# MLP layer two: the sixth block product of three chunks as seven small products for eight, and the second product by token tiles

## The chip, the cores and the metric

The kernel runs on one core of one Trainium2 chip. The metric is device time in microseconds (us) of that core; lower is better. The core has TensorE for matrix products (PE in the profile, PEld for its weight loads), VectorE (DVE), ScalarE (ACT), GpSimd (POOL) and SyncE (SP). DMAs are issued from the queues of SP, ACT and POOL. Each engine works through its own instructions in order; semaphores tie the engines to each other. PSUM has eight banks of 128 x 512 float32, into which TensorE writes.

## The reference, cut to what matters

The kernel computes one decoder layer for 512 tokens of width 2048. The change lies in the last part, a squared-ReLU MLP whose hidden width is 8192:

```
D_MODEL = 2048
SEQ = 512
D_FF = 4 * D_MODEL
...
        hn = rmsnorm(h, g_mlp[l])
        h = h + jnp.square(jax.nn.relu(hn @ w_ff1[l])) @ w_ff2[l]
    return rmsnorm(h, g_final)
```

"Layer two" below is the product with `w_ff2`: `u` (512 x 8192) times `w_ff2` (8192 x 2048), added to `h`.

## The kernel before, in words

**Precision.** Every float32 factor is split into a rounded part (`hi`, written by a ScalarE copy to the rounded type) and a remainder (`lo`, a VectorE subtraction). A product of two factors is three matmuls: hi by hi, hi by lo, lo by hi (`mm`, lines 1765 to 1767, each 128 x 128 by 128 x 512).

**Chunks and products.** Class `Mlp` does both layers. Layer two is cut into 8 chunks of 1024 hidden features. A chunk is a product of (512 tokens x 1024) by (1024 x 2048), done as a 2 x 2 x 2 block product with seven block products in place of eight (Winograd's form of Strassen's scheme). The products are numbered n = 0 to 6 in a chunk, and p counts them through both layers (`NP` = 56 in each). A block product is 256 tokens by 512 features by 1024 outputs: four weight tiles ("units", j = 0 to 3) of 128 x 1024, and for each of them two token tiles by two banks by three matmuls. So a unit is 12 matmuls, a product 48, a chunk 336.

**Where results go.** `USE` says for each n into which set of four PSUM banks it accumulates (X: four `mm` banks, for n = 0, 2, 4, 6; Y: three `st` banks and the `o` bank, for n = 1, 3 and, begun afresh, 5) and into which quarter of the output it is added after the product. A set is not cleared between its products: n = 2 goes on from n = 0, and so forth. `use2` (lines 1797 to 1804) adds the four banks to the residual rows in SBUF, four VectorE operations of 128 x 512, issued after the last unit of every product; the last of them waits for the last matmul.

**Weights.** `load` brings a unit from memory. For n = 0, 3 and 5 it is a plain load on SP's queue; for n = 1, 2, 4 and 6 it is a DMA on POOL's queue that adds the new block to a tile that is there already (the chain n = 0, 1, 2, 6 and the chain n = 3, 4), so such a DMA must wait until `low` has read the unit before it in its chain. `high` (line 1534) is the ScalarE cast of 128 x 1024, `low` (line 1539) the VectorE subtraction.

**Order of the work.** It is written out by hand in `run`. Before each unit i it calls `prep(i + FORE)` with `FORE` = 3, which puts into the queues: casts up to unit i + 4, remainders up to unit i + 3, loads up to unit i + 7. Then come, for the next product, the stationary factor (`stat` at j = 0: for n = 1 to 4 a VectorE sum of 128 x 1024, lines 1589 to 1595, and a ScalarE cast, line 1616; `stat_low` at j = 1: a VectorE subtraction, line 1621), the matmuls of the unit (`part`), and after j = 3 `use2`. On VectorE a product is thus: four remainders, for most n one sum, one `stat_low`, and four row additions, in that order, and nothing behind the row additions can start before the product's last matmul.

**Between the layers.** The results of layer one are transposed on TensorE into PSUM (`u_T`, line 1830), copied to one of four half tiles by ScalarE (`copies`, line 1839) and sent to memory by a DMA on ACT's queue (line 1840); layer two reads them back as its token factor. The last five of these copies fall into the first product of layer two and the start of its second. Its second product (p = `NP` + 1) begins a Y set whose fourth bank, `o`, was the last of the transposes' banks. `part` takes token tile 0 (banks 0 and 1) and then token tile 1 (banks 2 and 3) of each unit.

**Buffers.** Tiles of 128 x 1024 come from a list of 40 slots and 12 areas lent to it; `plain` takes the one that has been free for longer. A load waits until the slot's last reader is done.

Of the kernel before, what the change touches and what calls it, by code (L numbers as in the profile page):

```python
# [14 lines left out]
S, D, DFF, MEM = 512, 2048, 8192, 256  # L15
# [1443 lines left out]
class Mlp:  # L1459
# [14 lines left out]
    SIDE = ((0, 0), None, None, None, None, (0, 1), (1, 1))  # L1474
    CH = 8
    NP = 7 * CH
    TAG, TAG1 = "f2", "f1"
    FORE = 3
    ONE = False
    LAST = (5, 0, 1, 2, 3, 4, 6)  # L1480
    DONE = {0: (0, 0), 4: (1, 1)}

    def at(self, p):

        c, n = divmod(p - self.NP if p >= self.NP else p, 7)
        return c, self.LAST[n] if self.in_last(p) else n

    def in_last(self, p):
        return p >= 2 * self.NP - 7

    def begin(self, k):
        self.k, self.nc, self.W = k, k.nc, k.W
        self.raw, self.hl, self.chain, self.third = {}, {}, {}, {}
        self.S, self.sums, self.m = {}, {}, None
        self.nl = self.nh = self.no = 0
        self.units = 4 * (self.NP + 7 * self.CH)

    def __init__(self, k):
        self.begin(k)
# [11 lines left out]


    def load(self, i):
        p, j = divmod(i, 4)
        layer = p >= self.NP
        c, n = self.at(p)
        h, b = ((0, 0), (0, 1), (1, 1), (1, 1), (0, 1), (1, 0), (1, 0))[n]
        tag = (self.TAG, 8 * c + 4 * h + j, b) if layer else (self.TAG1, c, h, b, j)
        src = self.W.src(tag) if self.W.order is not None else None
        if n in (0, 3, 5):  # L1520
            t = self.k.slots.plain()
            (self.nc.gpsimd if self.ONE else self.nc.sync).dma_start(t, src)
            if n == 0:
                self.chain[j] = t
            elif n == 3:
                self.third[j] = t
        else:
            t = (self.third if n == 4 else self.chain)[j]
            self.nc.gpsimd.dma_start(t, src, accum_op=OP.add)  # L1529
        self.raw[i] = t  # L1530

    def high(self, i):
        t = HL(self.k.slots.get(), self.k.slots.get())
        self.nc.scalar.copy(t.hr, self.raw[i])  # L1534
        self.hl[i] = t

    def low(self, i):
        t, r = self.hl[i], self.raw.pop(i)
        self.nc.vector.tensor_sub(t.lr, r, t.hi)  # L1539
        if self.in_last(i // 4) and self.at(i // 4)[1] == 2:  # L1540
            self.load(i + 12)
        if self.at(i // 4)[1] >= 4:
            self.k.put(r)

    def loads(self, upto):
        while self.nl < upto:
            if not self.in_last(self.nl // 4) or self.at(self.nl // 4)[1] != 6:
                self.load(self.nl)
            self.nl += 1

    def prep(self, i):

        n = self.units
        self.loads(min(i + 2, n))
        while self.nh < min(i + 2, n):
            self.high(self.nh)
            self.nh += 1
        while self.no < min(i + 1, n):
            self.low(self.no)
            self.no += 1  # L1560
        self.loads(min(i + 2 + LOADS, n))


    def block(self, c, a):
        if c < self.CH:
            t = self.k.slots.plain()
            self.A[a] = [t]
            self.nc.sync.dma_start(t, self.k.d_u[c, a[1], a[0]].rearrange("p k n -> p (k n)"))

    def blocks(self, p):  # L1570

        if p < self.NP - 1:
            return
# [74 lines left out]
    def side(self, p, step):  # L1648

        if p > 7 * self.CH - 1:  # L1650
            return
# [25 lines left out]
    def run(self, out):  # L1677
        k = self.k
        if self.W.order is None:
            self.W.log += [("f1", c, h, b, i) for c in range(8) for h in range(2) for b in range(2) for i in range(4)]  # L1680
            self.W.log += [("f2", t, h) for t in range(DFF // 128) for h in range(2)]
            self.W.log += [(n, t, h) for n in ("wo", "w2") for t in range(KT) for h in range(2)]
            self.W.log += [("gs", c, h, b, i) for c in range(2) for h in range(2) for b in range(2) for i in range(4)]
        self.C, self.out = {}, out
        X = Y = None
        last = 2 * self.NP - 1
        for p in range(last):
            n, layer = self.at(p)[1], p // self.NP
# [5 lines left out]
            if n in (1, 5):  # L1694
                Y = [k.new_st() if p > 6 else k.new_mm() for _ in range(min(nb, 3))] + [k.new_o() for _ in range(nb - 3)]
            ps = (X, Y)[which]
            nh = 1 if p + 1 >= self.NP else 2
            for j in range(4):
                i = 4 * p + j
                self.copies()  # L1700
                self.prep(i + self.FORE)
                if j == 0:
                    self.blocks(p + 1)
                if j == 1 and p in (self.NP - 7, self.NP - 4, self.NP + 2, self.NP + 4):
                    self.res_in({-7: 0, -4: 1, 2: 2, 4: 3}[p - self.NP])
                if j % 2 == 0 and j // 2 < nh:
                    self.stat(p + 1, j // 2)
                if j % 2 and j // 2 < nh:
                    self.stat_low(p + 1, j // 2)
                while self.jobs and (self.jobs[0][0] <= i or i == 4 * self.NP + 3):  # L1710
                    self.jobs.popleft()[1]()
                if self.in_last(p):
                    if n in (1, 2) and j == 1:
                        self.gain(n - 1, 0)
                    if n == 4 and j in (1, 2):
                        for q in range(2):
                            self.square(j - 1, 2 + q)
                self.part(p, j, ps, range(2))
                if p == 0 and j < 2:
                    for d in (0, 1):  # L1720
                        self.x_in(12 + 2 * j + d, k.new_mm())
                if p == 0 and j == 3:
                    self.square(2, 2)
                    self.square(3, 2)
                if p == 1:
                    self.square(j, 3)
                if p == 2 and j == 2:
                    self.r = self.rstd(range(4), "rx3")
                if p == last - 14 and j == 0:
                    self.gain_rows()  # L1730
            if p == last - 1:
                self.prep(4 * last + 3)
# [8 lines left out]
        self.end(last, X, r)  # L1741

    def part(self, p, j, ps, ts):

        n = self.at(p)[1]
        B = self.hl[4 * p + j]
# [164 lines left out]

    def part3(self, p, j, i, ps):

        S, B, o = self.S[p, 0][0], self.hl[4 * p + j], 256 * j + 128
        self.mm(ps, S[:, o:o + 128], B[:, 512 * i:512 * i + 512], False, j == 3)

    def gain_rows(self):
# [36 lines left out]
class Gates(Mlp):  # L1954

    CH = 2
    ONE = True
    NP = 7 * CH
    TAG1 = "gs"
# [81 lines left out]
class Mixed(Mlp):  # L2041

    CH = 2
    NP = 0
    TAG = "wo"
    FORE = 4
    EARLY = 2
    ONE = True

# [119 lines left out]
class Out(Mlp):  # L2169

    CH = 2

    def in_last(self, p):
        return False
# [2 lines left out]
    HALF = 0.5  # L2177
    ONE = True
    TAG = "w2"
# [176 lines left out]
```

## Time and profile before

| | us |
|---|---|
| median of 3 runs | 2788.04 (2785.69 to 2788.9) |
| profiled execution, its own time | 2789.09 |
| its span, first to last instruction | 2787.3 |

| engine | busy us | share of the span | instructions |
|---|---|---|---|
| DVE | 2034.2 | 73% | 3217 |
| ACT | 1592.3 | 57% | 2670 |
| POOL | 530.9 | 19% | 796 |

The page of the profile gives busy time, the chain of work that ended last, and groups of instructions by line. Views of the trace used below are the waits (who waited for whom: total, times, longest), the timeline (start, duration, engine, line, operation, out<-in, count, and in brackets the idle time before it and who ended that), the windows (one line for a stretch: its length, then busy time and count of PE, PEld, DVE, ACT and POOL, the granted clock, the DMA share, GB/s) and the groups by shape. Tile names are the program's: `st`, `mm`, `o` are PSUM banks, `s`, `d` and `PP` are slots, `wts` is the weights in memory. In the timeline, a merged line (x4) shows the time from the first start to the last end.

### The profile page before, as it was taken

How to read it: one execution, taken by the hardware profiler on the slowest of the kernel's cores; microseconds unless marked ns; L12 is line 12 of the kernel's file. 1: busy time of each engine (PE TensorE's matmuls, PEld its weight loads, DVE VectorE, ACT ScalarE, POOL GpSimd, SP SyncE). 2: the span in 40 equal slices, each digit the busy share in tenths (PEclk: the TensorE clock that was granted, in tenths of full speed). 3: DMA queues.
4: the chain of work that ended last, by engine and by line, in shares of the span. 5: the costliest groups of instructions: out<-in, count | busy, mean ns of one | idle time of the engine just before them, and what ended most of it. 6: DMA issues, size and time to landing. Idle time of an engine off the chain costs nothing.

```text
span 2787.3 us, 37036 instructions
## 1 busy us (share of the span) xinstructions
PE 2765.3 (99%) x13428; PEld 2325.0 (83%) x13428; DVE 2034.2 (73%) x3217; ACT 1592.3 (57%) x2670; POOL 530.9 (19%) x796
## 2 busy tenths in 40 slices
PE   9999999999999999999999999999999999999998
PEld 8888889988888888888888888888888788888887
DVE  6347776766557886878866877777777788888888
ACT  5345556655557675556555766666666444444445
POOL 4021011011116232222200112111211121111111
PEclk9999999999999999999999999999999999999999
DMA  5331112222235798989814899888889998888986
GB/s 180 99 90 62 59 59 67 69 73 80 92 109 177 188 235 202 223 225 255 214 46 135 197 224 219 203 206 218 196 220 254 247 216 220 215 218 220 240 236 156
DMA packets 153383, 476.89 MB, mean 171 GB/s; under 512 B 15728, under 2 KB 40432, under 8 KB 153200
## 3 DMA queue, kind: packets, MB, share of 16 engines
q0 software_dynamic: 63616, 230.72, 39.8%
q1 hardware_dynamic: 71744, 226.25, 23.4%
q10 hardware_dynamic: 17840, 17.57, 1.9%
q8 instruction: 105, 1.72, 0.2%
q14 instruction: 78, 0.64, 0.1%
HBM read 443.01 MB, written 31.46 MB: 170 GB/s over the span
## 4 chain that ended last, share of the span: by engine, by line
PE 92%; DVE 3%; DMA 2%; ACT 2%; issue 1%; POOL 0%; DVEq 0%; ACTq 0%; POOLq 0%
PE mm L1767 10%; PE mm L1766 10%; PE mm L1765 10%; PE mm L437 9%; PE mm L439 8%; PE mm L438 8%; PE st L1767 7%; PE st L1765 7%; PE st L1766 7%; PE st L675 2%; PE o L1765 1%; PE o L1766 1%; PE o L1767 1%; PE st L438 1%; PE st L439 1%
## 5 line engine op out<-in xcount | busy, mean ns | idle before, releaser
L1765 PE MATMUL mm<-s,s 128*128 128x512 f32 x1392 | 545.4, 392 | 0.0
L1767 PE MATMUL mm<-s,s 128*128 128x512 f32 x1392 | 542.4, 390 | 1.1 <-DVE s L1621 1.0
L1766 PE MATMUL mm<-s,s 128*128 128x512 f32 x1392 | 541.8, 389 | 0.0
L1534 ACT CAST s<-d 128x1024 fp32r<-128x1024 f32 x272 | 282.3, 1050 | 245.7 <-DMA d<-wts 224.7
L437 PE MATMUL mm<-s,s 128*128 128x512 f32 (+5 forms) x1012 | 400.5, 396 | 0.0
L1539 DVE TENSOR_TENSOR s<-d,s 128x1024 fp32r<-128x1024 f32 x272 | 329.5, 1220 | 94.2 <-ACT s L1534 93.6
L1539 DVE TENSOR_TENSOR s<-s,s 128x1024 fp32r<-128x1024 f32 x252 | 304.9, 1221 | 105.4 <-ACT s L1534 103.3
L439 PE MATMUL mm<-s,s 128*128 128x512 f32 (+5 forms) x1012 | 381.6, 377 | 0.0
L438 PE MATMUL mm<-s,s 128*128 128x512 f32 (+5 forms) x1012 | 381.1, 377 | 0.0
L1534 ACT CAST s<-s 128x1024 fp32r<-128x1024 f32 x252 | 260.2, 1050 | 182.3 <-DMA s<-wts 161.5
L1765 PE MATMUL st<-s,s 128*128 128x512 f32 x920 | 360.6, 392 | 0.0
L1767 PE MATMUL st<-s,s 128*128 128x512 f32 x920 | 358.3, 389 | 0.0
L1766 PE MATMUL st<-s,s 128*128 128x512 f32 x920 | 358.1, 389 | 0.0
L1767 PEld LDWEIGHTS mm<-s,s 128*128 128x128 f32 x1392 | 261.3, 188 | 56.9 <-DVE s L1621 2.4
L1766 PEld LDWEIGHTS mm<-s,s 128*128 128x128 f32 x1392 | 261.4, 188 | 53.3
L1765 PEld LDWEIGHTS mm<-s,s 128*128 128x128 f32 x1392 | 261.4, 188 | 53.2 <-ACT s L1616 0.3
L1529 POOL DMA_DIRECT2D d<-wts x169 | 149.4, 885 | 813.1 <-DVE s L1539 662.3
L445 DVE TENSOR_TENSOR s<-s,s 128x512 fp32r<-128x512 f32 (+4 forms) x301 | 207.7, 700 | 94.9 <-ACT s L444 93.5
L444 ACT CAST s<-st 128x512 fp32r<-128x512 f32 (+4 forms) x249 | 112.3, 460 | 186.7 <-PE st L675 118.1
L439 PEld LDWEIGHTS mm<-s,s 128*128 128x128 f32 x1012 | 190.0, 188 | 32.6
L444 ACT CAST s<-s 128x512 fp32r<-128x512 f32 (+4 forms) x301 | 177.1, 603 | 59.6 <-PE mm L439 30.4
L437 PEld LDWEIGHTS mm<-s,s 128*128 128x128 f32 x1012 | 191.1, 189 | 20.9
(415 smaller groups left out, 4846.7 us busy)
## 6 DMA issues: line engine op xcount, KB each, us to landing
s<-wts SPq DMA_DIRECT2D x203, 512.0 KB, 3.7
d<-wts POOLq DMA_DIRECT2D x203, 512.0 KB, 8.2
s<-wts POOLq DMA_DIRECT2D x156, 512.0 KB, 8.2
d<-wts SPq DMA_DIRECT2D x69, 512.0 KB, 7.7
PP<-wts POOLq DMA_DIRECT2D x65, 512.0 KB, 8.5
d_u<-s ACTq DMA_DIRECT2D x64, 256.0 KB, 5.0
PP<-wts SPq DMA_DIRECT2D x27, 512.0 KB, 6.5
s<-d_u SPq DMA_DIRECT2D x16, 512.0 KB, 11.8
```

The costliest lines, as they stand in the source:

```text
L437: t.matmul(ps, a.hr, b.hr, start=first, stop=False)
L438: t.matmul(ps, a.hr, b.lr, start=False, stop=False)
L439: t.matmul(ps, a.lr, b.hr, start=False, stop=last)
L444: nc.scalar.copy(o.hr, src)
L445: nc.vector.tensor_sub(o.lr, src, o.hi)
L675: nc.tensor.transpose(ps[:rows, i * 128:i * 128 + 128], p, self.ident)
L1529: self.nc.gpsimd.dma_start(t, src, accum_op=OP.add)
L1534: self.nc.scalar.copy(t.hr, self.raw[i])
L1539: self.nc.vector.tensor_sub(t.lr, r, t.hi)
L1765: m(ps, a.hr, b.hr, start=first, stop=False, skip_group_check=True)
L1766: m(ps, a.hr, b.lr, start=False, stop=False, skip_group_check=True)
L1767: m(ps, a.lr, b.hr, start=False, stop=last, skip_group_check=True)
```

## The change

In chunks 0, 2 and 4 of layer two (`QUICK`) the sixth block product (n = 5) is itself done as a 2 x 2 x 2 block product of 128 tokens by 256 features by 512 outputs with seven sub-products. A sub-product is two weight half tiles by three matmuls, 6 matmuls; seven of them are 42.

- `sub_load` brings the four weight quarters in place of the four units, each as two DMAs of half a row, on SP's queue, nine units further ahead.
- `sum` puts four more VectorE operations of 128 x 1024 into the queue, the sums of quarters. Seven units, not four, then pass `high` and `low`. `prep`'s unit numbers run evenly over the chunk (`even`): 31 units in 55 steps of 6 matmuls.
- `stat_sums` makes four sums of 128 x 256 of the token factor on VectorE; `stat_hi2` casts them (ScalarE, 128 x 1024), `stat_lo2` is their remainder (VectorE, 128 x 1024).
- `swift` issues the sub-products: number 0 between units 2 and 3 of n = 4, numbers 1 to 5 in the place of n = 5, number 6 after the first unit of n = 6. Two results are carried on in PSUM: ScalarE copies bank a to b after sub-product 0 and b to f after sub-product 1, and later sub-products accumulate on the copies. Six row additions (`late2`), not four, are issued by `settled` a sub-product later.
- The second product of layer two (p = `NP` + 1) does token tile 0 of units 0, 1 and 2 before token tile 1 of unit 0.
- `Gates`, `Mixed` and `Out`, which inherit from `Mlp`, get `QUICK = ()` and keep their order.

```diff
+    QUICK = (0, 2, 4)
+    SUB = ((0, 0), (0, 1), (1, 1), (1, 0))
...
+    def even(self, p, j):
+
+        c = p - p % 7
+        if p < self.NP or not self.quick(c + 5):
+            return self.u0[p] + j
+        n = p % 7
+        t = 2 * (4 * n + j) if n < 5 else 40 + j if n == 5 else 47 + 2 * j
+        return self.u0[c] + 31 * t // 55
...
     def load(self, i):
-        p, j = divmod(i, 4)
+        p, j = self.U[i]
+        if i + 9 < len(self.U) and self.quick(self.U[i + 9][0]) and self.U[i + 9][1] < 4:
+            self.sub_load(*self.U[i + 9])
+        if self.quick(p):
+            return
...
+    def sum(self, i):
...
+        if j == 0:
+            B = [Q[p, i] for i in range(4)]
+            raw[u], raw[u + 3], raw[u + 5] = B[0], B[3], B[2]
+            raw[u + 2] = self.k.slots.plain()
+            v.tensor_sub(raw[u + 2], B[1], B[0])
+            raw[u + 4] = B[1]
+            v.tensor_sub(B[1], B[2], B[1])
+        elif j == 1:
+            raw[i] = self.k.slots.plain()
+            v.tensor_add(raw[i], Q[p, 1], Q[p, 0])
+            Q[p, 4] = raw[i]
+        elif j == 4:
+            raw[u + 6] = Q[p, 3]
+            self.turn4 = lambda: v.tensor_sub(Q[p, 3], Q[p, 3], Q[p, 4])
...
     def prep(self, i):
...
+        while self.nq < min(i + 4, n):
+            self.sum(self.nq)
+            self.nq += 1
...
-                self.prep(i + self.FORE)
+                self.prep(self.even(p, j) + self.FORE)
...
+                if j == 3 and p + 2 < last and self.quick(p + 2):
+                    self.stat_sums(p + 2)
+                if j > 1 and self.quick(p + 1):
+                    (self.stat_hi2 if j == 2 else self.stat_lo2)(p + 1)
+                self.settled()
...
-                self.part(p, j, ps, range(2))
+                if p == self.NP + 1:
+                    self.part(p, j, ps, [0])
+                    for i in (2, 3) if j == 3 else ():
+                        self.part(p, i - 1, ps, [1])
+                    if j > 1:
+                        self.part(p, j if j == 3 else 0, ps, [1])
+                else:
+                    self.part(p, j, ps, range(2))
+                if j == 2 and self.quick(p + 1):
+                    Y = [k.new_st() for _ in range(3)] + [k.new_o()]
+                    fast = self.swift(p + 1, Y)
+                    next(fast)
+                if p and j == 0 and self.quick(p - 1):
+                    next(fast, None)
...
+    def swift(self, p, ps):
...
+        plan = ((sub(0, 0), a, True, None, b), (com(1), b, False, (0, 1), f), (com(0), e, True, (1, 1), None),
+                (sub(0, 1), a, False, (0, 0), None), (com(2), f, False, (1, 1), None),
+                (com(3), e, False, (0, 1), None), (sub(1, 1), f, False, (1, 0), None))
+        for j, (l, o, start, at, to) in enumerate(plan):
+            self.prep(self.even(p, j) + self.FORE)
...
+            self.settled()
+            B = self.hl[self.u0[p] + j]
+            for q in range(2):
+                self.mm(o, l[q], B[:, 512 * q:512 * q + 512], start and q == 0, q == 1)
+            if to is not None:
+                nc.scalar.copy(to, o)
+            k.put(B.hi, B.lo)
+            if at:
+                r = self.row(*at)
+                self.late2.append(lambda o=o, r=r: v.tensor_add(r, o, r))
```

More of the change, by code (lines that the diff above doesn't have):

```diff
@@ L1494, in begin, with quick @@
         self.S, self.sums, self.m = {}, {}, None
-        self.nl = self.nh = self.no = 0
-        self.units = 4 * (self.NP + 7 * self.CH)
+        self.nl = self.nq = self.nh = self.no = 0
+        self.U, self.u0 = [], []
+        for p in range(self.NP + 7 * self.CH):
+            self.u0.append(len(self.U))
+            self.U += [(p, j) for j in range(7 if self.quick(p) else 4)]
+        self.units = len(self.U)
+        self.Q, self.late2 = {}, deque()
+    def quick(self, p):
+        return p >= self.NP and not self.in_last(p) and self.at(p)[1] == 5 and self.at(p)[0] in self.QUICK
+    def even(self, p, j):
[5 more added lines that the diff above has]
+        return self.u0[c] + 31 * t // 55
     def __init__(self, k):
@@ L1693, in run @@
                 X = [k.new_mm() if p else k.new_st() for _ in range(nb)]
-            if n in (1, 5):
+            if n == 1 or n == 5 and not self.quick(p):
                 Y = [k.new_st() if p > 6 else k.new_mm() for _ in range(min(nb, 3))] + [k.new_o() for _ in range(nb - 3)]
@@ L1697, in run @@
             nh = 1 if p + 1 >= self.NP else 2
+            if self.quick(p):
+                for _ in range(5):
+                    next(fast)
+                continue
             for j in range(4):
@@ L1731, in run @@
             if p == last - 1:
-                self.prep(4 * last + 3)
+                self.prep(self.units - 1)
                 r = self.rstd([0, 1], meanwhile=lambda: self.use2(p, ps))
@@ L1741, in run, with stat_sums @@
         self.end(last, X, r)
+    def stat_sums(self, p):
+        g = self.nc.vector
+        x = self.A[0, 1][0].rearrange("p (k n) -> p k n", k=4)
+        t = self.k.slots.plain()
+        s = [t[:, 256 * i:256 * i + 256].rearrange("p (k n) -> p k n", k=2) for i in range(4)]
+        a = {(h, kk): x[:, 2 * kk:2 * kk + 2, 128 * h:128 * h + 128] for h in range(2) for kk in range(2)}
+        g.tensor_add(s[0], a[1, 0], a[1, 1])
+        g.tensor_sub(s[1], s[0], a[0, 0])
+        g.tensor_sub(s[2], a[0, 0], a[1, 0])
+        g.tensor_sub(s[3], a[0, 1], s[1])
+        self.S[p, 1] = t
@@ new lines, in stat_hi2, with stat_lo2 @@
+    def stat_hi2(self, p):
+        t = self.S[p, 1]
+        x = HL(self.k.slots.get(), self.k.slots.get())
+        self.nc.scalar.copy(x.hr, t)
+        self.S[p, 1] = (x, t)
+    def stat_lo2(self, p):
+        x, t = self.S[p, 1]
+        self.nc.vector.tensor_sub(x.lr, t, x.hi)
+        self.k.put(t)
+    def swift(self, p, ps):
+        nc, k = self.nc, self.k
+        v = nc.vector
+        A, Z = self.S[p, 0][0], self.S[p, 1][0]
+        a, e, f, b = ps
+        sub = lambda t, kk: [A[:, 256 * (2 * kk + q) + 128 * t:256 * (2 * kk + q) + 128 * t + 128] for q in range(2)]
+        com = lambda i: [Z[:, 256 * i + 128 * q:256 * i + 128 * q + 128] for q in range(2)]
+        plan = ((sub(0, 0), a, True, None, b), (com(1), b, False, (0, 1), f), (com(0), e, True, (1, 1), None),
[3 more added lines that the diff above has]
+            self.prep(self.even(p, j) + self.FORE)
+            if j == 2:
+                self.blocks(p + 1)
+                self.stat(p + 1, 0)
+            if j == 4:
+                self.stat_low(p + 1, 0)
+            self.settled()
+            B = self.hl[self.u0[p] + j]
+            for q in range(2):
+                self.mm(o, l[q], B[:, 512 * q:512 * q + 512], start and q == 0, q == 1)
[5 more added lines that the diff above has]
+                self.late2.append(lambda o=o, r=r: v.tensor_add(r, o, r))
+            if j == 6:
+                k.put(A.hi, A.lo, Z.hi, Z.lo)
+            yield
@@ L1956 @@
     CH = 2
+    QUICK = ()
     ONE = True
@@ L2043 @@
     CH = 2
+    QUICK = ()
     NP = 0
@@ L2171 @@
     CH = 2
+    QUICK = ()
     def in_last(self, p):
```

37 lines of the change are left out of this document (32 added, 5 removed).

## The prediction

> **What bounds the kernel now.** I read the page first, then the waits of PE, then the windows of single chunks of layer two, then the timeline of VectorE and ScalarE inside them.
>
> ```profile
> span 2787.3 us, 37036 instructions
> PE 2765.3 (99%) x13428; PEld 2325.0 (83%) x13428; DVE 2034.2 (73%) x3217; ACT 1592.3 (57%) x2670; POOL 530.9 (19%) x796
> PE 92%; DVE 3%; DMA 2%; ACT 2%; issue 1%; POOL 0%; DVEq 0%; ACTq 0%; POOLq 0%
> ```
>
> TensorE is busy throughout and is the chain that ends last, so a matmul fewer, or a wait more, moves the end one for one. The next view is the window of chunk 2 of layer two, from its first matmul to that of chunk 3.
>
> ```profile
> 2320.75:2396.91 76.16, 76.16 (x337) 63.06 (x336) 63.67 (x68) 34.68 (x35) 14.08 (x16) 1.00 0.89 221
> ```
>
> PE has no gap in it: 336 matmuls of its own in 76.16 us are 0.2267 us each, a unit of 12 is 2.72, a product of 48 is 10.88. The clock is full. VectorE is busy for 63.67 us; it has 12.5 us to spare in a chunk, ScalarE 41.
>
> The one wait of PE that the change aims at is in the second product of layer two (waits of PE, then the timeline):
>
> ```profile
> PE o L1765 <- ACT s L1839: 2.2, 1, 2.2
> ```
> ```profile
> 2176.82 0.39 PE L1765 MATMUL st<-s,s 128*128 128x512 f32 x1
> 2180.58 0.58 ACT L1839 COPY s<-o 128x512 f32<-128x512 f32 x1 [5.83 <-DMA d_u<-s]
> 2181.22 0.50 PE L1765 MATMUL o<-s,s 128*128 128x512 f32 x1 [2.19 <-ACT s L1839]
> 2201.07 0.39 PE L1765 MATMUL st<-s,s 128*128 128x512 f32 x1
> ```
>
> The product starts at 2176.82, comes to the `o` bank after 9 matmuls, and waits 2.19 us for ScalarE's copy out of it, which itself waited for a DMA to free its half tile. The last row is the first matmul of n = 3 of chunk 0.
>
> **The change part by part.**
>
> *Matmuls.* Three products lose 6 matmuls each: 3 x 6 x 0.2267 = 4.08 us, 1.36 a chunk.
>
> *Second product.* Token tile 0 of three units (18 matmuls) and the first bank of tile 1 (3) now lie ahead of the `o` bank: 2176.82 + 21 x 0.2267 = 2181.58, and the copy ends at 2181.16. The wait of 2.19 goes, with 0.4 us to spare; bounds 0 to 2.19, should the DMA land later.
>
> So at best 6.27 us go. What is added is work for VectorE. Its prices, by groups of shape (the last two rows, of 128 x 256 and of ScalarE's copies, are of other stages):
>
> ```profile
> L1539 DVE TENSOR_TENSOR s<-d,s 128x1024 fp32r<-128x1024 f32 x106 | 127.7, 1219 | 21.3 <-ACT s L1534 21.1
> L1589 DVE TENSOR_TENSOR s<-s,s 128x1024 f32<-128x1024 f32 x5 | 6.1, 1219 | 0.0
> L1804 DVE TENSOR_TENSOR s<-s,mm 128x512 f32<-128x512 f32 x48 | 32.1, 686 | 10.7 <-PE mm L1767 10.7
> L1306 DVE TENSOR_TENSOR s<-mm,s 128x256 f32<-128x256 f32 x4 | 1.7, 418 | 0.9 <-PE mm L439 0.9
> L1839 ACT COPY s<-o 128x512 f32<-128x512 f32 x61 | 35.2, 577 | 5.8 <-DMA d_u<-s 5.8
> ```
>
> Back to back they cost less than they last, as the timeline of n = 3 and n = 4 of chunk 2 shows:
>
> ```profile
> 2349.12 1.22 DVE L1539 TENSOR_TENSOR s<-d,s 128x1024 fp32r<-128x1024 f32 x1
> 2351.55 2.73 DVE L1804 TENSOR_TENSOR s<-s,mm 128x512 f32<-128x512 f32 x4 [1.21 <-PE mm L1767]
> 2354.20 1.22 DVE L1539 TENSOR_TENSOR s<-s,s 128x1024 fp32r<-128x1024 f32 x1
> 2355.33 1.22 DVE L1595 TENSOR_TENSOR s<-d,s 128x1024 f32<-128x1024 f32 x1
> 2356.47 1.22 DVE L1539 TENSOR_TENSOR s<-d,s 128x1024 fp32r<-128x1024 f32 x1
> 2362.29 1.23 DVE L1539 TENSOR_TENSOR s<-d,s 128x1024 fp32r<-128x1024 f32 x1 [2.20 <-ACT s L1534]
> 2363.43 1.88 DVE L1802 TENSOR_TENSOR s<-st,s 128x512 f32<-128x512 f32 x3
> 2365.23 0.68 DVE L1802 TENSOR_TENSOR s<-o,s 128x512 f32<-128x512 f32 x1
> 2365.90 2.36 DVE L1539 TENSOR_TENSOR s<-s,s 128x1024 fp32r<-128x1024 f32 x2
> ```
> ```profile
> 2353.39 0.39 PE L1765 MATMUL st<-s,s 128*128 128x512 f32 x1
> ```
>
> Wide operations (128 x 1024) start 1.135 us apart (2354.20, 2355.33, 2356.47). Four row additions that need not wait take 2365.90 - 2363.43 = 2.47, 0.62 each. A small sum lies between 0.34 (its 0.42 less the overlap of 0.085) and 0.42; I take 0.34, as its operands are all in SBUF. VectorE cannot run ahead over a product's end: its row additions wait for the last matmul, and it is free 0.81 us after the next product's start (2353.39 to 2354.20).
>
> In one of the three chunks VectorE gets: three more remainders, one remainder of the token sums, four sums of quarters (8 x 1.135 = 9.1), four small sums (1.35), two more row additions (1.2): 11.65 us. 63.67 + 11.65 = 75.3, and PE would need only 74.80. Most of it falls into n = 3 and n = 4, where the 12.5 us to spare are not to be had.
>
> So I follow VectorE's queue from T, the start of n = 3, by the order in which `run` fills it (units counted in the chunk, `even` applied):
>
> - n = 3: remainder 16, sum for n = 4, two sums of quarters, remainder 17, `stat_low`, third sum, remainders 18 and 19, four small sums; four row additions of n = 3
> - n = 4: remainders 20, 21, 22, `stat_low`, remainder 23, fourth sum, remainders 24, 25, `stat_lo2`; four row additions of n = 4
> - n = 5: remainder 26, addition of sub-product 1, remainder 27, addition of sub-product 2, which frees bank e
>
> PE needs `stat_lo2` for the third matmul of sub-product 1: T + 10.88 + 8.16 (three units) + 1.36 (sub-product 0) + 2.72 (unit 3) + 0.45 = T + 23.57. VectorE has by then 18 wide operations, the small sums and four row additions to do: T + 0.81 + 20.4 + 1.35 + 2.5 = T + 25.1. PE waits 1.5 us. Sub-product 5 accumulates on bank e, so it must wait for the addition that reads it: without waits PE is there at T + 28.56. VectorE: 20 wide, 10 row additions, the small sums: T + 0.81 + 22.7 + 6.2 + 1.35 = T + 31.06. **All in all PE waits 2.5 us per chunk** (of which 1.5 are the first wait), against 1.36 saved: +1.14 in chunks 2 and 4. After that there is room: n = 6 has no sum, and the next chunk is an ordinary one.
>
> In chunk 0 PE is 2.19 us earlier, but VectorE is not, since remainder 11 of n = 2 is tied to a DMA:
>
> ```profile
> 2189.87 2.00 ACT L1534 CAST s<-d 128x1024 fp32r<-128x1024 f32 x2 [2.01 <-DMA d<-wts]
> 2191.43 1.22 DVE L1539 TENSOR_TENSOR s<-d,s 128x1024 fp32r<-128x1024 f32 x1
> ```
>
> Its cast starts at 2189.87 because the DMA lands then; the remainder can start at 2190.95; seven wide operations (remainders 11 to 15, sum and `stat_low`) and four row additions bring VectorE to 2201.37. T is 2201.07 - 2.19 = 2198.88, so VectorE is free at T + 2.49, not T + 0.81: 1.68 later. PE waits 4.18: -1.36 - 2.19 + 4.18 = +0.63. **Most of the second product's gain is given back in the same chunk.**
>
> Sum: 0.63 + 1.14 + 1.14 = +2.9 us.
>
> *What I cost at nothing.* ScalarE: four more casts and three copies a chunk, some 6 us of its 41. The copy a to b must end before T + 23.12; ahead of it in its queue lie nine casts after that of unit 19.
>
> ```profile
> 2364.82 2.00 ACT L1534 CAST s<-s 128x1024 fp32r<-128x1024 f32 x2 [2.56 <-DMA s<-wts]
> 2367.67 2.95 ACT L1534 CAST s<-s 128x1024 fp32r<-128x1024 f32 x3
> ```
>
> At 0.95 us apart they end at about 2365.8 + 9 x 0.95 = 2374.4, T + 21.0; with 0.58 (the copies' row above; between 0.3 and 1.05) T + 21.6, 1.5 us in time, and the copy b to f has two sub-products as cover. The half loads carry the same bytes and start nine units (24 us) earlier on SP's queue; the loads of n = 3 stand behind them there. If that cover fails, it shows as a late remainder (second rival).
>
> [...]
>
> **The rivals.**
>
> *One: it is hidden.* If VectorE gets through n = 3 and n = 4 without PE waiting, 4.08 + 2.19 = 6.3 us go: 2782.8 in the profiled execution. For it: VectorE idles 12.5 us a chunk. Against: that idle time lies ahead of n = 3, behind row additions that wait for PE. Half of it would be 2786.
>
> *Two, slower: the fourth DMA of n = 4.* In the new order remainder 19 stands ahead of n = 3's row additions and of everything that sub-product 0 needs, so each us by which its data come after VectorE is ready is a us of PE. VectorE is ready for it at T + 0.81 + 8 x 1.135 = T + 9.89. Before, it started at 2365.90 in chunk 2 (T + 9.89 = 2363.28) and, in chunks 0 and 4, here:
>
> ```profile
> 2215.52 1.23 DVE L1539 TENSOR_TENSOR s<-s,s 128x1024 fp32r<-128x1024 f32 x1 [0.17 <-ACT s L1534]
> 2517.59 2.35 DVE L1539 TENSOR_TENSOR s<-s,s 128x1024 fp32r<-128x1024 f32 x2
> 2505.71 0.39 PE L1765 MATMUL st<-s,s 128*128 128x512 f32 x1
> 2355.82 0.87 POOL L1529 DMA_DIRECT2D s<-wts  x1 [4.20 <-DVE s L1539]
> ```
>
> If the landings stay, 2.6 us are added in chunk 2, 2.0 in chunk 4 (T = 2505.71), 5.1 in chunk 0: +9.7, together +12.6 or 2801.7. It is slower by more than can be told from nothing once a third of this comes true. Against: the last row, where that DMA's issue in chunk 2 waits for remainder 15, which now stands ahead of n = 2's row additions, behind the remainder of 2349.12, and can start at 2350.3 and not 2354.20; and the loads of n = 5 have left that stretch.
>
> *Three: full durations.* At 1.22 and 0.69 instead of 1.135 and 0.62 the sum grows by 20 x 0.085 + 10 x 0.07 = 2.4 a chunk, and 0.9 more in chunk 0: +8.1, together +11, 2800.1.
>
> *Four: the change does not do what it says.* The `o` bank comes free later, as half loads share the DMA engines with the transposes' writes, and PE waits there as before. By the sum for chunk 0 this costs next to nothing more, as VectorE sets the time there: 2792.
>
> **How the numbers follow.** The profiled execution took 2789.09 (span 2787.3, 1.8 around it), 1.05 more than the median of the runs, 2788.04. The forecast is 2789.09 + 2.9 = 2792.0 in its terms, 2791.0 as a median; its own range, with small sums and overlaps at their bounds, 2788 to 2795. Chances: forecast 0.47, hidden 0.2, the DMA 0.23, full durations 0.05, no effect on the wait 0.05. Two in a thousand, 5.6 us, is about what a measurement can tell from no change here: faster means below 2782.5, which only the whole of the first rival reaches, 0.1; slower means above 2793.6, most of the second and third rivals, 0.28; between them 0.62. The range from 2783 to 2799 leaves out the whole of the first rival and the worst of the others.
>
> **What would show it.** In the changed profile: 18 matmuls fewer, no wait of 2.2 on the copy at `o`; new waits of PE on VectorE of about 1.5 us at sub-product 1 and 1 us at sub-product 5 in each of the three chunks, some 1.7 more in chunk 0; VectorE without idle time from the start of n = 3 until sub-product 5. If PE shows no such waits, my queue is wrong; if VectorE waits at remainder 19 for a cast that waits for a DMA, it is the second rival; if wide operations start 1.22 apart, the third.

## The result, and the profile after

The kernel after takes 2805.01 us (median of 6 runs, 2803.23 to 2806.87), the kernel before 2788.47 in the same series: a ratio of 1.0060, with a 95% interval from 1.0047 to 1.0073. It is 16.5 us slower, where 2.9 us were forecast, and it lies outside the range. The profiled execution of after took 2803.23 us, the fastest of its six; what the profile shows is that one execution.

The page of after, its span and busy time:

```profile
span 2801.5 us, 37069 instructions
PE 2768.3 (99%) x13410; PEld 2322.6 (83%) x13410; DVE 2064.4 (74%) x3259; ACT 1606.9 (57%) x2688; POOL 531.0 (19%) x796
```

The 18 matmuls are gone (13428 to 13410), and the span is 14.2 us longer. The windows of chunks 0, 2 and 4 of after, each from its first matmul to that of the next chunk, say where:

```profile
2164.18:2247.76 83.58, 79.64 (x349) 64.53 (x348) 72.65 (x80) 42.49 (x47) 13.22 (x15) 0.98 0.88 225
2323.92:2405.29 81.37, 77.70 (x331) 62.76 (x330) 72.97 (x81) 38.54 (x40) 13.21 (x15) 0.98 0.83 206
2481.45:2563.16 81.71, 77.65 (x331) 62.82 (x330) 72.81 (x81) 38.60 (x40) 13.21 (x15) 0.98 0.84 205
```

Before, these chunks took 80.58, 76.16 and 76.16. The differences, 3.00, 5.21 and 5.55, are 13.76 of the 14.2 us. The chunks between them still take 76.16. What PE waits for in after (its waits from 2100 us to the end):

```profile
PE st L1919 <- DVE s L1690: 8.7, 3, 2.9
PE st L1917 <- DVE d L1886: 1.8, 3, 0.6
PE o L1982 <- ACT s L1991: 0.8, 1, 0.8
PE mm L1919 <- DVE s L1690: 0.6, 2, 0.4
PE st L1918 <- DVE s L1594: 0.3, 2, 0.2
```

The wait of 2.2 at the `o` bank in the second product is gone (L1982 is the transposes of layer one's results). In its place PE waits 2.9 us in each of the three chunks for a `stat_low` (L1690), and 0.6 for the addition that frees bank e (L1886). Both are VectorE's. The next two fences show where VectorE lost its time in chunk 2: its timeline, and the matmul with which n = 3 starts, T.

```profile
2343.32 1.23 DVE L1594 TENSOR_TENSOR s<-PP,s 128x1024 fp32r<-128x1024 f32 x1 [1.27 <-ACT s L1589]
2347.08 1.22 DVE L1594 TENSOR_TENSOR s<-d,s 128x1024 fp32r<-128x1024 f32 x1 [2.53 <-ACT s L1589]
2348.22 1.88 DVE L1954 TENSOR_TENSOR s<-st,s 128x512 f32<-128x512 f32 x3
...
2358.63 2.47 DVE L1956 TENSOR_TENSOR s<-s,mm 128x512 f32<-128x512 f32 x4
2361.02 1.22 DVE L1594 TENSOR_TENSOR s<-s,s 128x1024 fp32r<-128x1024 f32 x1
```
```profile
2356.56 0.39 PE L1917 MATMUL st<-s,s 128*128 128x512 f32 x1
```

VectorE comes to n = 2's row additions at 2358.63, 1.9 us after their matmuls, and is free at 2361.02, T + 4.46; the forecast had T + 0.81. The idle time lies earlier, ahead of remainders whose casts are late. Summed over the products n = 0 to 2 of chunk 2 (waits of VectorE in before, then in after):

```profile
DVE s L1539 <- ACT s L1534: 1.1, 1, 1.1
```
```profile
DVE s L1594 <- ACT s L1589: 5.4, 4, 2.5
```

ScalarE, which makes the casts, in turn waits for add-on DMAs (its waits in the same two stretches, before, then after):

```profile
ACT s L1534 <- DMA d<-wts: 7.7, 4, 3.0
```
```profile
ACT s L1589 <- DMA d<-wts: 12.1, 4, 5.3
ACT s L1589 <- DMA PP<-wts: 1.6, 1, 1.6
```

The DMA view of 30 us from the same place of the chunk, before and then after, has busy tenths of the DMA engines in 40 slices, what they moved, and per kind of issue the median time to landing:

```profile
DMA  9979943799999999999999999950000966068679
DMA packets 1398, 5.10 MB, mean 170 GB/s; under 512 B 160, under 2 KB 160, under 8 KB 1395
d<-wts POOLq DMA_DIRECT2D x5, 512.0 KB, 6.9
```
```profile
DMA  9999999999999999999999999999999950000001
DMA packets 2097, 6.59 MB, mean 220 GB/s; under 512 B 240, under 2 KB 240, under 8 KB 2093
d<-wts POOLq DMA_DIRECT2D x4, 512.0 KB, 10.0
```

After has no gap for 24 us, then moves next to nothing for 5: half loads, the loads of n = 3 and the add-ons of n = 1 and n = 2 stand in one heap, and an add-on takes 10.0 us to land and not 6.9 (medians of the rows shown).

### The profile page after: what moved, and what is told of

Its sections match the earlier page's. It is cut to its first block, busy times and chain, and to the rows that moved or that the text cites. A ratio compares the mean times of both kernels' runs of the same rounds, so it can differ in the third digit from the quotient of the medians.

```text
span 2801.5 us, 37069 instructions
## 1 busy us (share of the span) xinstructions
PE 2768.3 (99%) x13410; PEld 2322.6 (83%) x13410; DVE 2064.4 (74%) x3259; ACT 1606.9 (57%) x2688; POOL 531.0 (19%) x796
## 5 line engine op out<-in xcount | busy, mean ns | idle before, releaser
L1589 ACT CAST s<-s 128x1024 fp32r<-128x1024 f32 x285 | 294.9, 1049 | 228.2 <-DMA s<-wts 193.8
L1594 DVE TENSOR_TENSOR s<-s,s 128x1024 fp32r<-128x1024 f32 x285 | 344.6, 1220 | 108.3 <-ACT s L1589 107.9
L1589 ACT CAST s<-d 128x1024 fp32r<-128x1024 f32 x247 | 257.0, 1050 | 213.4 <-DMA d<-wts 190.8
L1594 DVE TENSOR_TENSOR s<-d,s 128x1024 fp32r<-128x1024 f32 x247 | 299.6, 1219 | 96.9 <-ACT s L1589 96.0
L1919 PEld LDWEIGHTS mm<-s,s 128*128 128x128 f32 x1392 | 262.1, 188 | 58.5 <-DVE s L1690 3.7
L1918 PEld LDWEIGHTS mm<-s,s 128*128 128x128 f32 x1392 | 262.6, 189 | 53.8
L1917 PEld LDWEIGHTS mm<-s,s 128*128 128x128 f32 x1392 | 262.5, 189 | 53.4
L1552 POOL DMA_DIRECT2D d<-wts x153 | 135.3, 884 | 794.1 <-DVE s L1594 555.4
L439 PEld LDWEIGHTS mm<-s,s 128*128 128x128 f32 x1012 | 190.0, 188 | 34.2 <-DVE s L448 1.7
L1919 PEld LDWEIGHTS st<-s,s 128*128 128x128 f32 x920 | 172.9, 188 | 45.8 <-DVE s L1690 9.7
```

The lines of the kernel that those rows point to most:

```text
L439: t.matmul(ps, a.lr, b.hr, start=False, stop=last)
L1917: m(ps, a.hr, b.hr, start=first, stop=False, skip_group_check=True)
L1918: m(ps, a.hr, b.lr, start=False, stop=False, skip_group_check=True)
L1919: m(ps, a.lr, b.hr, start=False, stop=last, skip_group_check=True)
```

## The experiments

All chunk lengths are read from the trace as above. "Time" is the median where there were several runs, else the one run. Chunk 0 starts between 2162.5 and 2166.4 us in these profiles: what lies ahead of it differs by up to 4 us, so the chunks are the better measure.

| kernel | time | chunk 0 | chunk 2 | chunk 4 |
|---|---|---|---|---|
| before | 2788.47 | 80.58 | 76.16 | 76.16 |
| after | 2805.01 | 83.58 | 81.37 | 81.71 |
| tiles_only, tiles_again | 2786.69, 2787.86 | 78.36, 78.09 | 76.16 | 76.16 |
| no_sums | 2797.55 | 83.35 | 80.31 | 77.47 |
| loads13 | 2802.61 | 85.26 | 80.62 | 81.01 |
| lead_late | 2806.36 | 85.24 | 81.61 | 82.82 |
| loads4 | 2793.78 | 80.62 | 79.46 | 78.65 |
| low_first | 2806.12 | 86.12 | 81.75 | 80.87 |
| pool_sums | 2833.56 | 93.57 | 90.48 | 91.51 |
| combo | 2820.42 | 90.22 | 87.42 | 85.92 |
| loads4_no_sums | 2788.97 | 79.20 | 78.53 | 75.20 |
| early_token | 2791.93 | 78.96 | 77.71 | 76.67 |
| by_due | 2792.47 | 79.40 | 77.85 | 75.81 |

The letters of the theories hold within one expectation each.

**The second product alone** (tiles_only, and tiles_again in five rounds).

```diff
-    QUICK = (0, 2, 4)
+    QUICK = ()
```

> The second product by token tiles alone (QUICK is empty). Theory A, the wait at the o bank was all there was to it: chunk 0 of layer two takes 80.58 - 2.19 = 78.4 us from its first matmul to that of chunk 1, the other chunks 76.16, the kernel 2.2 us less than before. Theory B, the first weights of layer two, tied to DMAs, hold PE up later in the same chunk: chunk 0 stays above 79.5 and PE waits for VectorE there.

> The second product by token tiles alone (QUICK empty), once more, in five rounds. The run of three rounds gave 2786.69 and a ratio of 0.9993, its interval from 0.9983 to 1.0003. Theory: the wait of 2.19 us at the o bank is gone and nothing else moves, so 2.2 us less, a ratio of 0.9992; an interval of five rounds may or may not leave 1 out. If the 2.2 us came only by chance in that run, chunk 0 would take 80.5 us again.

Chunk 0 takes 78.36 and 78.09 in place of 80.58, 2.2 and 2.5 us less, and the other chunks stay at 76.16. The gain is there in the trace. In the times it cannot be told from nothing: ratios 0.9993 (0.9983 to 1.0003) and 0.9996 (0.9987 to 1.0005).

**The sums of quarters left out** (no_sums; quarters go in their place, all the rest of the change stays).

```diff
-            v.tensor_sub(raw[u + 2], B[1], B[0])
-            raw[u + 4] = B[1]
-            v.tensor_sub(B[1], B[2], B[1])
+            raw[u + 2] = raw[u + 4] = B[1]
```

> The changed kernel without its four sums of weight quarters (the quarters themselves go in their place; the result is another): 4.5 us of VectorE work fewer in each of the three chunks, same matmuls, same loads, same casts. Theory A, VectorE's queue sets the time from the start of n = 3 on: the three chunks lose some 2 us against their matmuls (6.6 in the changed kernel), chunk 2 takes 76.5 to 77.5 us, not 81.4. Theory B, PE waits for something that does not depend on the amount of VectorE work (the order of the token factor, bank copies, DMAs): chunk 2 stays at 80 us or more.

Chunk 4 comes down by 4.2 us, chunk 2 only by 1.1, chunk 0 by 0.2. That the 4.2 is near the 4 x 1.135 that the sums cost is in part luck. VectorE is free 0.9 us earlier there (T + 3.90 and not T + 4.81), though the sums lie behind that point. From there to the addition that frees bank e it takes 3.4 us less: the sums' 4.5 less 1.20 that it now idles ahead of remainder 19. In chunk 2 VectorE stands 3.01 us idle there, since the add-on DMA is late, and in chunk 0 a wait of 2.4 us at the second product's `o` bank is back:

```profile
PE o L1908 <- ACT s L1982: 2.4, 1, 2.4
```

So the sums are a part of the loss, and late DMAs another.

**Half loads thirteen units ahead** (loads13).

```diff
-        if i + 9 < len(self.U) and self.quick(self.U[i + 9][0]) and self.U[i + 9][1] < 4:
-            self.sub_load(*self.U[i + 9])
+        if i + 13 < len(self.U) and self.quick(self.U[i + 13][0]) and self.U[i + 13][1] < 4:
+            self.sub_load(*self.U[i + 13])
```

> The half loads start 13 units ahead, not 9, so that they land before the add-on DMAs of n = 1 and n = 2. Theory A, the half loads delay these add-ons, and through them remainders 10 and 11, so that VectorE comes late to n = 3: VectorE ends its row additions of n = 2 about 1 us after the start of n = 3 (4.5 in the changed kernel), chunk 2 takes 77 to 78.5 us, not 81.4. Theory B, VectorE is late for another reason: chunk 2 stays within 1 us of 81.4.

Within 0.8 us of after in chunks 2 and 4, and chunk 0 worse: by its numbers theory B. But loading the halves still earlier does not clear the stretch. All eight are now issued ahead of chunk 2, and the loads of n = 3 stand among the add-ons of n = 1 and n = 2 instead; VectorE is free at T + 3.71 in chunk 2 and T + 4.10 in chunk 4. The run does not tell the two theories apart.

**The queue's lead put off** (lead_late).

```diff
         n = p % 7
+        if n < 3:
+            return self.u0[p] + j
```

> The lead of `even` begins at n = 3, so remainders 10 and 11 stand behind the row additions of n = 1, as before the change. Theory A, the DMAs are late and VectorE waits for them in either order: VectorE is free 3 to 4 us after the start of n = 3, chunk 2 takes 80 to 81.5 us. Theory B, the order is at fault, a remainder that waits for a DMA ahead of row additions that need not: VectorE is free at most 1.5 us after that start, chunk 2 takes 77.5 to 78.5 us.

No gain. VectorE is free at T + 3.24 in chunk 2, inside theory A's 3 to 4 us, but one more wide operation now lies behind that point: from there to the addition that frees bank e it takes 31.76 us and not 30.48. That `prep` runs ahead of the ordinary order in the first three products is not what costs the time.

**Half loads four units ahead** (loads4).

```diff
-        if i + 9 < len(self.U) and self.quick(self.U[i + 9][0]) and self.U[i + 9][1] < 4:
-            self.sub_load(*self.U[i + 9])
+        if i + 4 < len(self.U) and self.quick(self.U[i + 4][0]) and self.U[i + 4][1] < 4:
+            self.sub_load(*self.U[i + 4])
```

> The half loads are issued four units ahead, not nine, so that they stand behind the loads of n = 3 on SP's queue and not between them. Theory A (VectorE comes to n = 3 late because the add-on DMAs of n = 1 and n = 2 share the DMA engines with half loads and loads of n = 3 issued at 2321 to 2335 us): the add-ons of n = 1 and n = 2 land as early as before, VectorE is free at about T + 0.8 in chunk 2 in place of T + 4.46, the first wait of PE falls from 2.9 to 0.5 at most, and chunks 2 and 4 take 77.3 to 78.5 us in place of 81.4 and 81.7: about 2797. Rival B (the order of the loads is not what makes the add-ons late; the faster running ahead of the queue is): VectorE still free at T + 4 or later, chunks 81 to 82, about 2804. If the halves land too late, VectorE idles ahead of the first quarter sum, and that shows there.

This one edit takes 2.96, 1.91 and 3.06 us off the chunks, 7.9 of the 13.76 by which they had grown. (The one run's time is 11.2 us under after's median, but 1.5 of that lies ahead of layer two, and after's profile is 1.8 below its own median.) Chunk 4 of this run: its windows row, the waits of VectorE in n = 0 to 2, its timeline, and PE's first matmuls of n = 3 and of sub-product 5.

```profile
2475.09:2553.74 78.65, 75.97 (x332) 61.63 (x330) 72.89 (x81) 38.74 (x40) 13.24 (x15) 1.00 0.88 213
```
```profile
DVE s L1594 <- ACT s L1589: 2.7, 2, 2.3
```
```profile
2507.07 2.47 DVE L1956 TENSOR_TENSOR s<-s,mm 128x512 f32<-128x512 f32 x4
2509.47 1.22 DVE L1594 TENSOR_TENSOR s<-d,s 128x1024 fp32r<-128x1024 f32 x1
```
```profile
2507.72 0.39 PE L1917 MATMUL st<-s,s 128*128 128x512 f32 x1
...
2540.00 0.50 PE L1917 MATMUL st<-s,s 128*128 128x512 f32 x1 [0.58 <-DVE d L1886]
```

VectorE is free at 2509.47, T + 1.75 (chunk 2: T + 2.54; chunk 0: T + 1.78). The expectation's T + 0.8 and its 77.3 were not reached in any chunk: half of the lateness in chunk 2 stays, and there add-ons still land late (DMA view, 30 us from the same place of chunk 2):

```profile
d<-wts POOLq DMA_DIRECT2D x5, 512.0 KB, 9.4
s<-wts SPq DMA_DIRECT2D x8, 256.0 KB, 9.7
```

The half loads still share the engines with the last add-ons of n = 2; issued behind them they were not tried. But the place of the half loads is shown to be the larger cause: with nine or thirteen units VectorE is free at T + 3.2 or later in chunks 2 and 4 of all six kernels (from one kernel to the next the same chunk differs by up to 1.9 us), with four and the order otherwise kept at T + 1.6 to T + 2.5 (loads4, combo, loads4_no_sums).

**The late remainder put first** (low_first).

```diff
                 self.copies()
+                early = j == 1 and self.quick(p + 1)
+                if early:
+                    self.stat_low(p + 1, 0)
                 self.prep(self.even(p, j) + self.FORE)
```

> The remainder of n = 5's token factor (stat_low) is put ahead of remainders 21 and 22 in VectorE's queue, nothing else changes. Theory A (the end of VectorE's queue, the addition that frees bank e, sets the length of the chunk, and the halved clock lies inside time that PE would wait anyway): the first wait falls from 2.9 by 2.27 us to 0.6, the granted clock stays at 1, the wait at sub-product 5 grows, and chunks 2 and 4 stay at 81 to 82 us: 2804 to 2806. Rival C (the wait at sub-product 0 and the halved clock behind it are what costs): chunks 2 and 4 come down by 2.5 to 4 us each, to 77.5 to 79: about 2797.

Chunk 4 of this run, waits of PE in its timeline:

```profile
2539.51 0.50 PE L1922 MATMUL st<-s,s 128*128 128x512 f32 x1 [1.77 <-DVE s L1690]
2544.61 0.50 PE L1920 MATMUL o<-s,s 128*128 128x512 f32 x1 [1.20 <-ACT o L1885]
2546.45 0.50 PE L1922 MATMUL o<-s,s 128*128 128x512 f32 x1 [1.11 <-DVE s L1858]
2552.31 0.50 PE L1920 MATMUL st<-s,s 128*128 128x512 f32 x1 [0.58 <-DVE d L1889]
```

The first wait falls to 1.77 and not to 0.6, new ones come behind it, and sub-product 5 still waits for bank e. Chunks 2 and 4 change by +0.38 and -0.84, where rival C said 2.5 to 4 us less; the -0.84 is VectorE's earlier start (T + 3.95 and not T + 4.81), since from there to bank e it takes 30.48 us, as in after. (In chunk 0 a wait of 2.7 us at the second product's `o` bank came back; that is most of its +2.54.) PE's longest wait is not what sets the chunk's length; the end of VectorE's queue is.

**The sums on GpSimd** (pool_sums; combo adds loads4 and low_first to it, three rounds).

```diff
-        v, Q, raw, u = self.nc.vector, self.Q, self.raw, self.u0[p]
+        v, Q, raw, u = self.nc.gpsimd, self.Q, self.raw, self.u0[p]
```

> The four sums of quarters are done by GpSimd and no longer by VectorE. GpSimd's nearest row is 1.48 us for 128 x 512 of float32, so some 2.9 us for a sum of 128 x 1024 (estimate), 11.6 us for the four, between the issues of n = 4's and n = 6's add-on DMAs. Theory A (VectorE's queue is too long by the sums' 4.5 us and the lateness of 3.65): VectorE is through 4.5 us earlier, as in the run without the sums; chunk 4 takes 77 to 78, chunk 2 79 to 80.5 with VectorE idle ahead of remainder 19, chunk 0 81 to 83.5: 2796 to 2799. Rival D (GpSimd's sums come late, or slow VectorE's operations down while both work): PE waits for the second or third sum's unit at sub-products 2 to 4, or wide VectorE operations start more than 1.2 us apart beside a sum; then 2803 or more.

> The three edits together: half loads four units ahead, sums of quarters on GpSimd, the remainder of n = 5's token factor ahead of remainders 21 and 22. Theory A: both causes are gone, chunks 2 and 4 take 75 to 76.2 us (74.80 is the bound of the matmuls), chunk 0 76 to 78.5 in place of 80.58 before: 2781 to 2786, a ratio of 0.997 to 0.999 to the kernel before. Rival B or D (an add-on DMA or a GpSimd sum still comes late): chunks 2 and 4 77 to 80, 2787 to 2795.

Slower by far: chunks of 90 to 94 us in pool_sums and 86 to 90 in combo, whose ratio is 1.0106 (1.0088 to 1.0125). Rival D came true. The timelines of VectorE and of GpSimd in chunk 4 of pool_sums:

```profile
2540.58 2.53 DVE L1594 TENSOR_TENSOR s<-s,s 128x1024 fp32r<-128x1024 f32 x1
2543.03 3.42 DVE L1664 TENSOR_TENSOR s<-PP,s 128x1024 f32<-128x1024 f32 x1
2546.37 3.39 DVE L1594 TENSOR_TENSOR s<-s,s 128x1024 fp32r<-128x1024 f32 x1
```
```profile
2539.28 2.73 POOL L1576 TENSOR_TENSOR s<-PP,d 128x1024 f32<-128x1024 f32 x1
2542.10 3.27 POOL L1578 TENSOR_TENSOR PP<-s,PP 128x1024 f32<-128x1024 f32 x1
2545.44 3.23 POOL L1581 TENSOR_TENSOR s<-PP,d 128x1024 f32<-128x1024 f32 x1
...
2562.83 5.49 POOL L1585 TENSOR_TENSOR s<-s,s 128x1024 f32<-128x1024 f32 x1 [14.15 <-DVE s L1594]
```

Beside the three sums VectorE's operations take 2.53, 3.42 and 3.39 us and not 1.22. Each ends 1.1 us after the GpSimd sum beside it (2543.11 after 2542.01, 2546.45 after 2545.37, 2549.76 after 2548.67), as if it had begun only when the sum was over; why was not shown. The sums take 3.4 us off VectorE and cost it 5.7 us. The fourth sum, beside a busy VectorE, takes 5.49 us itself, where the first three took 2.73 to 3.27. ScalarE's cast of it comes next, the copy a to b stands behind that cast, and PE waits 4.4 us for the copy.

**Both causes taken away** (loads4_no_sums: the edits of loads4 and of no_sums).

> Half loads four units ahead and, besides, the four sums of quarters left out (quarters go in their place, so the sub-products are not those of the reference). With the half loads alone moved, chunks 2 and 4 took 79.46 and 78.65 us, 4.66 and 3.85 over the 74.80 of the matmuls alone. Theory A (two causes that add up: the late add-on DMAs, and more VectorE operations between the start of n = 3 and sub-product 5 than fit): the second is gone as well, 4 x 1.135 = 4.54 us of VectorE, and chunks 2 and 4 come to 74.8 to 75.6, chunk 0 to 77 to 78.5: 2783 to 2786. Rival E (what is left in PE's waits are landings of DMAs, or the copies between banks, and not VectorE's count): chunks 2 and 4 stay over 77.

Windows of chunks 2 and 4, and VectorE ahead of remainder 19 in chunk 2:

```profile
2319.02:2397.55 78.53, 75.69 (x332) 61.71 (x330) 68.37 (x77) 38.66 (x40) 13.22 (x15) 1.00 0.87 213
2473.71:2548.91 75.20, 75.14 (x332) 61.88 (x331) 68.36 (x77) 39.63 (x41) 13.21 (x15) 1.00 0.91 223
```
```profile
2363.73 1.23 DVE L1588 TENSOR_TENSOR s<-s,s 128x1024 fp32r<-128x1024 f32 x1 [3.88 <-ACT s L1583]
```

In chunk 4 the two together account for nearly all: alone loads4 gave 3.06 us and no_sums 4.24, together they give 6.51 of the 6.91 that lie between after and the matmuls alone (81.71 to 74.80). In chunk 2 VectorE has time enough and then stands idle for 3.88 us: the second rival of the prediction, which the sums had covered. In chunk 4 it idles 1.25 us there. Why the cast ahead of remainder 19 comes later in chunk 2 was not followed further.

**Work moved into VectorE's idle time, and in the order in which it is due** (early_token, by_due; both on top of loads4). In early_token the token factor's small sums, cast and remainder move from n = 3 and n = 4 to n = 1:

```diff
                 self.copies()
+                far = j == 2 and p + 4 < last and self.quick(p + 4)
+                if far:
+                    self.stat_sums(p + 4)
+                    self.stat_hi2(p + 4)
                 self.prep(self.even(p, j) + self.FORE)
...
-                if j == 3 and p + 2 < last and self.quick(p + 2):
-                    self.stat_sums(p + 2)
-                if j > 1 and self.quick(p + 1):
-                    (self.stat_hi2 if j == 2 else self.stat_lo2)(p + 1)
+                if far:
+                    self.stat_lo2(p + 4)
```

by_due adds the edit of low_first, and `settled` ahead of `prep` in `swift`:

```diff
         for j, (l, o, start, at, to) in enumerate(plan):
+            self.settled()
             self.prep(self.even(p, j) + self.FORE)
```

> Half loads four units ahead, and the four small sums of the token factor, their cast and their remainder moved from n = 3 and n = 4 to n = 1 of the chunk, where VectorE idled 2.2 to 3.5 us ahead of a remainder whose cast waits for an add-on DMA; no operation is added or dropped. With the half loads alone moved, chunks 2 and 4 took 79.46 and 78.65. Theory A (what is left is VectorE's queue between the start of n = 3 and sub-product 5, and its idle time before n = 3 can be used): 1.35 + 1.14 = 2.5 us leave that queue, the wait for the token remainder at sub-product 1 goes, and chunks 2 and 4 take 76.2 to 77.5: about 2788 to 2790. Rival F (VectorE's idle time before n = 3 cannot be used, since the whole chunk has 75.3 us of VectorE's work against 74.8 of matmuls, so that the work moved ahead only makes it later at n = 3): chunks stay at 78.5 or more, about 2793.

> As the run before, and besides: the remainder of n = 5's token factor ahead of remainders 21 and 22, and in the sub-products the additions of the last result ahead of the next remainders. Theory A: by the queue, from VectorE free at T + 1.75 as in chunk 4 of the run with the half loads alone moved, the addition that frees bank e ends at about T + 28.4, and PE needs it at T + 28.56; the remainder of n = 6's token factor is 0.2 us late. Chunks 2 and 4 take 75 to 76, chunk 0 77 to 78, so the kernel takes 2 to 5 us less than before: 2783.5 to 2786.5, a ratio of 0.998 to 0.9993. Rival F or rival two (an add-on DMA of n = 4 late by itself): chunk 2 over 77.5, total 2787 or more.

The move is worth 1.66, 1.75 and 1.98 us a chunk, so idle time ahead of n = 3 can be used, though 2.5 us were moved. The order is worth 0.86 more in chunk 4. Chunks 0 and 2 are 0.44 and 0.14 longer with it, where VectorE was also free 0.54 and 0.24 us later. Windows of chunks 2 and 4 of by_due:

```profile
2320.30:2398.15 77.85, 75.74 (x331) 61.73 (x330) 72.89 (x81) 38.60 (x40) 13.22 (x15) 1.00 0.88 222
2474.31:2550.12 75.81, 75.12 (x332) 61.82 (x330) 72.81 (x81) 38.99 (x41) 13.22 (x15) 1.00 0.90 228
```

VectorE is busy for 72.8 to 72.9 us of each chunk, and the matmuls alone need 74.80. With 2 us to spare idle time soon shows: in chunk 2 it waited 1.50 and 0.51 for casts in n = 1 and was free at T + 3.63. Sub-product 5 no longer waits for bank e in any of the three chunks; in chunk 2 PE waits 1.2 us for the copy a to b, which stands behind the cast of VectorE's fourth sum, and 0.6 for the remainder of n = 6's token factor. Chunk 4 is at last shorter than an ordinary chunk, by 0.35; chunk 2 is not. In five rounds by_due stands at 1.0010 to before (1.0001 to 1.0019): no version with the sub-products that was tried beats before.

## Why the prediction was wrong

**The step that failed** is in the walk along VectorE's queue: "VectorE cannot run ahead over a product's end: its row additions wait for the last matmul, and it is free 0.81 us after the next product's start". That row came from before, where VectorE waited 1.21 us for PE at n = 2's row additions. In after PE is done first. VectorE is free at T + 4.46 in chunk 2, by the same reading at T + 4.81 in chunk 4, and at T + 4.69 in chunk 0, where T + 2.49 was forecast. The prediction named the edit that did it, and costed it at nothing: the half loads that "start nine units (24 us) earlier on SP's queue" with "the loads of n = 3" behind them. It looked for the damage at n = 4's fourth add-on; it lay at those of n = 1 and n = 2, as loads4 shows: with the half loads behind the loads of n = 3, VectorE is free at T + 1.78, T + 2.54 and T + 1.75. What keeps it from T + 0.81 then stays open. The prediction quotes no row of the DMA engines for that stretch, where before's are 90% busy or more in 24 of 40 slices already.

**The rest of the sum held.** From VectorE free to the end of the addition that frees bank e the forecast had 31.06 - 0.81 = 30.25 us. In after this addition is the first row here, 2390.82 + 0.68 = 2391.50, so 30.48 us from 2361.02 (timelines of VectorE and of PE):

```profile
2390.82 0.68 DVE L1886 TENSOR_TENSOR d<-st,d 128x512 f32<-128x512 f32 x1
```
```profile
2391.56 0.50 PE L1917 MATMUL st<-s,s 128*128 128x512 f32 x1 [0.60 <-DVE d L1886]
```

Put the measured start into the forecast's own sum, and the chunks come out within 0.5 us:

| chunk | forecast | later start | gives | measured |
|---|---|---|---|---|
| 0 | 80.58 + 0.63 | 4.69 - 2.49 = 2.20 | 83.41 | 83.58 |
| 2 | 76.16 + 1.14 | 4.46 - 0.81 = 3.65 | 80.95 | 81.37 |
| 4 | 76.16 + 1.14 | 4.81 - 0.81 = 4.00 | 81.30 | 81.71 |
| 4, loads4 | 76.16 + 1.14 | 1.75 - 0.81 = 0.94 | 78.24 | 78.65 |

So 9.85 of the 10.85 us by which the three chunks missed the forecast are this one term, and loads4 takes most of it away. VectorE's work in all was forecast too high, 75.3 us a chunk where 72.7 to 73.0 were measured; in part its operations overlap their neighbours more now, in chunk 2 by 5.2 us in all and not 3.1 (durations summed, less the time in which one or more ran). The time does not hang on that figure.

**Point by point.** *Matmuls:* right, 1.36 a chunk; chunk 4 of loads4_no_sums reaches 75.20. *Second product:* right in tiles_only and tiles_again, 2.2 and 2.5 us, and in after given back in the same chunk as said, and more. *The first wait:* its size and place were wrong, 1.5 at sub-product 1 against 2.9 at sub-product 0. By the prediction's own list `stat_low` stands behind remainders 20 to 22, while sub-product 0 needs it two matmuls in; only `stat_lo2` was held against its due time. By the prediction's own prices `stat_low` would be done at about T + 19.4 and due at T + 19.5, so from a start at T + 0.81 there would be no wait: this wait too is the late start. It made no difference to the sum (low_first). *Bank e:* right, as the place that sets the length. *The copy a to b:* its cover held in after, where PE had waited 2.9 us before; in low_first and in by_due PE waited 1.2 us for it. The prediction took ScalarE's casts as back to back, but the last cast ahead of the copy must wait for VectorE's fourth sum (6.26 us idle in after), so the copy is as late as VectorE is.

**The rivals.** *Hidden:* no. *The DMA of n = 4:* the kind of event was right, the place was wrong; it comes at n = 4 only once the sums are gone (3.01 and 3.88 us). *Full durations:* no, the queue's length rules them out: 30.48 us where 30.25 were forecast and 2.4 more would be needed. *The `o` bank as before:* no in after's profile, where the copy ended 0.24 us ahead of PE, but yes in all five others with the half loads nine or thirteen units ahead: PE waited there 2.4 (no_sums), 0.9 (loads13), 1.5 (lead_late), 2.7 (low_first) and 2.9 us (pool_sums). In the five with four units, and in the two without half loads, it did not wait. This speaks for the rival's mechanism, and against its price of next to nothing: chunk 0 was 1.7 to 2.5 us longer than after's in loads13, lead_late and low_first. Whether after's other executions hold that wait is not shown.

## What to carry to other kernels

An engine's start in a stretch is itself a result of what comes before it: when a change moves transfers, follow the transfers they share the DMA engines with back to the casts and remainders that wait for them, before a row of the old profile is taken for the start. Loads issued earlier were not free here: with the half loads nine units ahead the DMA engines had no gap for 24 us, and the add-ons, which were due first, took 10.0 us to land and not 6.9. And a faster product is worth no more than the room on the engine that feeds it: here VectorE got 9 us more work a chunk to save TensorE 1.36, and no order of that work that was tried made it pay.

## What the runs showed of the hardware

TensorE's granted clock fell to half at each of PE's three waits of 2.91 us at sub-product 0 in after, as the wait ended or within 1.5 us of its end (0.50 over the 3.40 us from 2223.80 in chunk 0, 0.50 over the 3.41 from 2380.80 in chunk 2, 0.52 over the 3.40 from 2537.70 in chunk 4). loads13 and lead_late have three such waits too, and a mean clock of 0.98 and 0.96 in chunk 2. Windows of chunk 2 of after, the wait, the stretch behind it and the next:

```profile
2376.49:2379.90 3.41, 0.50 (x2) 0.19 (x2) 3.41 (x4) 0.00 (x0) 0.00 (x0) 1.00 0.94 252
2380.80:2384.21 3.41, 3.41 (x10) 2.63 (x9) 3.38 (x4) 1.94 (x3) 0.00 (x0) 0.50 0.53 154
2384.21:2387.60 3.39, 3.39 (x16) 2.65 (x15) 3.39 (x6) 1.25 (x3) 0.00 (x0) 1.00 0.92 321
```

For 3.41 us a matmul takes 0.427 us and not 0.227, some 1.6 us for eight of them. It cost next to nothing in after, since VectorE's queue ended later anyway: the 30.48 us from VectorE's start to bank e are the same in chunk 4 of loads4, where the clock was 1.00. Where PE is nearly in time it could cost up to that 1.6 us (an estimate from the two matmul times). The length of a wait alone does not decide it: in low_first no wait at sub-products 0 and 1 was longer than 1.8 us, and the clock fell in chunk 2 and not in chunk 4 (windows of 3.40 us of the two):

```profile
2388.50:2391.90 3.40, 2.96 (x7) 2.38 (x8) 3.40 (x6) 0.85 (x2) 0.00 (x0) 0.50 1.00 398
2544.60:2548.00 3.40, 2.28 (x9) 1.58 (x10) 3.40 (x5) 1.25 (x2) 0.00 (x0) 1.00 0.85 269
```

What else decides it was not shown.

Not expected either: how long GpSimd's sums and VectorE's wide operations become beside each other, VectorE's 2.53 to 3.42 us and not 1.22, the fourth sum 5.49 (pool_sums, above).
